# Forgetting attention: two query blocks of a head finished together, one bias operation for all heads, and the shift's sign taken in where it is spread

## The chip, the core and the metric

The kernel runs on one core of one Trainium2 chip. The metric is device time in microseconds for one execution of the whole kernel, as the median of several runs. A core has five engines with a queue of instructions each: TensorE (PE, with its weight loads shown as PEld), VectorE (DVE), ScalarE (ACT), GpSimd (POOL) and SyncE (SP), which issues nearly all DMA transfers of this kernel. Queues run side by side and wait for each other through semaphores.

## The reference

One layer of a streaming encoder. 16 meta tokens are put in front of 2048 input tokens (T = 2064, width 1024). The layer normalises, projects to the inputs of three groups of heads (a linear recurrence, forgetting attention, RWKV-7), joins their outputs by an output projection, and adds a normalised result; then comes a gated feed-forward part with a short convolution. The change lies in the forgetting attention, 8 heads of 64 columns:

```
log_f = log_sigmoid(f_logit + f_bias)
c = cumsum(log_f)                                   # per head, over the tokens
s = q @ k^T / 8 + (c[query] - c[key]),  -inf where key > query
o = softmax(s) @ v
```

## The kernel before

**The stages.** The input projection comes first, in three parts of the tokens, with the recurrences beside it. Then `Attn.run` (lines 771 to 796) does the attention. The end of the last recurrence overlaps with its beginning, and the output projection (`w_out_tile`, line 1443, 17 tiles of up to 128 tokens) overlaps with its second half. The feed-forward part follows. The program is written in one order; the framework then plans each engine's queue from estimated durations (`schedule_with_timeline_sim=True`, line 2141), so that work written later can be put into gaps.

**The attention's blocks.** A block is one head and 512 queries: 8 heads times 4 query blocks b = 0 to 3, 32 blocks, after 16 meta queries that `meta` does apart. The first half of the stage does b = 0 and 1 of all heads, the second half b = 2 and 3; within a half, the two blocks of a head follow each other. Each block has three steps.

`maxima` (line 503) finds, for each of the 512 queries, the largest score. TensorE computes scores in pieces into banks called `mx` (line 527), VectorE reduces each piece (lines 530, 533) and then the pieces of a query (line 540) into `sh`, 128 partitions by 4. Line 541 negates that and subtracts the reference `cref` (the value of `c` at the block's first key tile). TensorE transposes the result (line 545) and `shift` (line 553) spreads it into four rows of the operand `q2`: row j holds the shift of queries 128 j to 128 j + 127 and zeros elsewhere, because it is multiplied with the unit matrix on the way. In the trace `q2` is called `q`. Line 548 makes the block's bias, `cref - ccol` for each of 17 key tiles.

`weights` (line 621) runs two blocks behind. For each tile of 128 keys TensorE computes scores transposed (`sc`, lines 653 and 654; `q2` and `k2` bring in shift and forgetting), ScalarE takes the exponential with the bias (line 658), GpSimd masks, and TensorE multiplies with the values into `po` (line 676). `po` holds two partial sums, in partitions 0 to 63 and 64 to 127. GpSimd and VectorE add up the weights in `acc` (line 697) for the denominators. While it does so, `fill` puts pieces of `maxima` of a later block between.

`ending` (line 702) finishes a block. The two halves of `po` are added into `o`, 64 partitions by 512 (lines 710 to 713). Then three steps are put off by `DELAYS` = 2, 7 and 12 ticks (a tick is a pair of key tiles): `total` sums `acc` over the partitions by matmul and stores 512 denominators to memory (line 726), and reads them back as 16 by 32 (line 727); `invert` takes the reciprocal (line 731), stores it (line 732) and reads it back spread over 64 partitions as `rb` (line 733); `scale` multiplies `o` by `rb` (line 736) and stores it to `scr["mix"]` (line 737), from which the output projection reads. The delayed steps that are still open at the end run after the last block.

**The order around it.** SyncE's queue issues the loads of `q` and `k` of later blocks, these stores and reads, and the loads of the output projection, in the planned order; an issue waits for what it needs and all behind it wait too. Tiles 7 and 8 of the output projection are held back (`HELD`, line 1858) until the last matmul of the second-last block, to have work for TensorE at the end. Tile i (from 1) covers tokens 16 + 128 (i - 1) onwards, so tiles 1 to 8 read blocks b = 0 and 1, tiles 9 to 12 read b = 2 and tiles 13 to 16 read b = 3, of all heads.

Of the kernel before, what the change touches and what calls it, by code (L numbers as in the profile page):

```python
# [8 lines left out]
F32 = mybir.dt.float32  # L9
# [3 lines left out]
AF = mybir.ActivationFunctionType  # L13
ALU = mybir.AluOpType
# [4 lines left out]
P = 128  # L19
# [306 lines left out]
NH = 8  # L326
NKT = 17
# [6 lines left out]
def attn_consts(core):  # L334
    nc = core.nc
    c = core.const

    core.future = c.tile([P, P], F32, name="future")
    nc.gpsimd.memset(core.future[:], 0.0)
    nc.gpsimd.affine_select(  # L340
        out=core.future[:], in_=core.future[:], compare_op=ALU.is_ge, fill=NEG, base=0,
        pattern=[[-1, P]], channel_multiplier=1,
    )
    core.ones_row = c.tile([1, P], F32, name="ones_row")
    nc.vector.memset(core.ones_row[:], 1.0)
    core.ccol = c.tile([P, NKT, NH], F32, name="ccol")
    nc.vector.memset(core.ccol[:], 0.0)
    core.cref = c.tile([P, NKT, NH], F32, name="cref")
    core.ctail = c.tile([NH, META], F32, name="ctail")
    nc.vector.memset(core.ctail[:], 0.0)  # L350
    core.ones_col = c.tile([P, 1], F32R, name="ones_col")
    nc.vector.memset(core.ones_col[:].bitcast(F32), 1.0)
    core.ones_64 = c.tile([META, 64], F32, name="ones_64")
    nc.vector.memset(core.ones_64[:], 1.0)
    core.ones_8 = c.tile([NH, 1], F32, name="ones_8")
    nc.vector.memset(core.ones_8[:], 1.0)

# [54 lines left out]
class Attn:  # L412
# [7 lines left out]
    def __init__(self, core, pool, psum, more, scr):  # L420
        self.core, self.pool, self.psum, self.more, self.scr = core, pool, psum, more, scr
        self.wide, self.bank, self.place = False, 0, 0
        nc = self.nc = core.nc
        self.clock, self.later, self.serial, self.added = 0, [], 0, 0
        self.pending, self.loads, self.steps = None, [], []


        self.turn = {"k": 1, "q2": 0, "q3": 0}
        self.ring = {s: [] for s in self.turn}
        for i in range(self.AHEAD + 1):  # L430
            q3 = pool.tile([P, 512], F32R, tag=f"q3_{i}", name=core.n("q3"), bufs=1)
            self.fixed(q3, None, self.ONES)
            self.ring["q3"].append(q3)
            q2 = pool.tile([P, 512], F32R, tag=f"q2_{i}", name=core.n("q2"), bufs=1)
            nc.vector.memset(q2[64:128].bitcast(F32), 0.0)
            self.ring["q2"].append(q2)
            if i > 1:
                continue
            k1 = pool.tile([P, 2, KHALF], F32R, tag=f"k1_{i}", name=core.n("k1"), bufs=1)
            k2 = pool.tile([P, 2, KHALF], F32R, tag=f"k2_{i}", name=core.n("k2"), bufs=1)  # L440
            v1 = pool.tile([P, 2, NKT // 2 + 1, 64], F32, tag=f"v1_{i}", name=core.n("v1"), bufs=1)
            self.fixed(None, k2, self.ONES)
            self.ring["k"].append((k1, k2, v1))
# [59 lines left out]
    def maxima(self, h, b, keys):  # L503

        nc, core, scr = self.nc, self.core, self.scr
        k1, k2, v1 = keys
        r = slice(64 * h, 64 * h + 64)
        t0, n, ref = META + 512 * b, 512, 4 * b
        qt = [(P * i, P, META + P * (4 * b + i)) for i in range(4)]
        ts = slice(t0, t0 + n)  # L510
        q3 = self.next("q3")
        q1 = self.t([P, 512], "q1", F32R, self.AHEAD + 1)
        q2 = self.next("q2")
        nc.sync.dma_start(q3[0:64, :n].bitcast(F32), scr["qh"][r, ts])
        nc.sync.dma_start(q1[0:64, :n].bitcast(F32), scr["qh"][r, ts])
        nc.sync.dma_start(q1[64:128, :n].bitcast(F32), scr["qh"][r, ts])
        nc.sync.dma_start(q2[0:64, :n].bitcast(F32), scr["ql"][r, ts])
        nq = len(qt)
        mc = self.t([P, 4, 6], "mc")
        nc.vector.memset(mc[:], NEG)  # L520
        for i, (qo, rows, prior) in enumerate(qt):
            for ci in range(len(MAX_CUTS) - 1):
                a, e = MAX_CUTS[ci], min(MAX_CUTS[ci + 1], prior + rows)
                if a >= e:
                    break
                ps = self.mx()
                nc.tensor.matmul(ps[:rows, : e - a], q3[:, qo : qo + rows], k2[:, a:e], start=True, stop=True)  # L527
                full = min(e, prior) - a
                if full > 0:
                    self.reduced = nc.vector.tensor_reduce(mc[:rows, i, ci : ci + 1], ps[:rows, :full], axis=AX.X, op=ALU.max)  # L530
                if e == prior + rows:
                    junk = self.t([P, P], "mj")
                    nc.vector.tensor_tensor_reduce(
                        junk[:rows, :rows], ps[:rows, full : full + rows], core.future[:rows, :rows],
                        1.0, NEG, ALU.add, ALU.max, mc[:rows, i, 5:6],
                    )
                yield None
        sh = self.t([P, 4], "sh")
        rows = qt[0][1]
        nc.vector.tensor_reduce(sh[:rows, :nq], mc[:rows, :nq], axis=AX.X, op=ALU.max)  # L540
        nc.vector.tensor_scalar(
            sh[:rows, :nq], sh[:rows, :nq], -1.0, core.cref[:rows, ref, h : h + 1], op0=ALU.mult, op1=ALU.subtract
        )
        ps = self.mx()
        nc.tensor.transpose(ps[:nq, :rows], sh[:rows, :nq], core.ident[:rows, :rows])
        self.shift(q2.rearrange("p (i q) -> p i q", q=P), ps[:nq, :rows])
        bias = self.t([P, NKT], "bias", bufs=self.AHEAD + 1)
        nc.vector.tensor_scalar(
            bias[:], core.ccol[:, :, h], -1.0, core.cref[:, ref, h : h + 1], op0=ALU.mult, op1=ALU.add
        )  # L550
        yield q1, q2, bias

    def shift(self, q2, rows):

# [66 lines left out]
    def weights(self, h, b, keys, queries, fill):  # L621
# [6 lines left out]
        nc, core, scr = self.nc, self.core, self.scr  # L628
        k1, k2, v1 = keys
        q1, q2, bias = queries  # L630

        t0, n = META + 512 * b, 512
# [69 lines left out]
        def ending(po, acc):  # L702


            while len(self.later) > 8:
                self.later.pop(0)[2]()

            o, oh = self.t([64, 512], "o", bufs=4), self.t([64, 512], "oh")
            c1 = kt[1][2]
            nc.scalar.activation(oh[:, c1:n], po[64:128, c1:n], AF.Copy)  # L710
            if c1:
                nc.scalar.activation(o[:, :c1], po[0:64, :c1], AF.Copy)
            nc.vector.tensor_tensor(o[:, c1:n], po[0:64, c1:n], oh[:, c1:n], op=ALU.add)
            g = n // 16
            dcol = self.t([16, 32], "dcol", bufs=4)
            rb = []

            def total():
                ah, al = (self.t([P, 512], "oh", F32R) for _ in range(2))
                nc.scalar.activation(ah[:, :n], acc[:, :n], AF.Copy)  # L720
                nc.gpsimd.tensor_tensor(al[:, :n], acc[:, :n], ah[:, :n], op=ALU.subtract)
                ps = self.mx()
                nc.tensor.matmul(ps[0:1, :n], core.ones_col[:], ah[:, :n], start=True, stop=False)
                nc.tensor.matmul(ps[0:1, :n], core.ones_col[:], al[:, :n], start=False, stop=True)
                nc.scalar.activation(acc[0:1, :n], ps[0:1, :n], AF.Copy)
                nc.sync.dma_start(scr["den"][h : h + 1, ts], acc[0:1, :n])
                nc.sync.dma_start(dcol[:, :g], scr["den"][h, ts].rearrange("(p c) -> p c", c=g))

            def invert():
                rb.append(self.t([64, 512], "rb"))  # L730
                nc.vector.reciprocal(dcol[:, :g], dcol[:, :g])
                nc.sync.dma_start(scr["rden"][h, ts].rearrange("(p c) -> p c", c=g), dcol[:, :g])
                nc.sync.dma_start(rb[0][:, :n], scr["rden"][h : h + 1, ts].broadcast_to([64, n]))

            def scale():
                nc.vector.tensor_tensor(o[:, :n], o[:, :n], rb[0][:, :n], op=ALU.mult)
                nc.sync.dma_start(scr["mix"][256 + 64 * h : 256 + 64 * h + 64, ts], o[:, :n])

            for d, f in zip(self.DELAYS, (total, invert, scale)):
                self.serial += 1  # L740
                self.later.append((self.clock + d, self.serial, f))
            self.later.sort(key=lambda x: x[:2])
# [1402 lines left out]
```

## Time and profile before

| what | value |
|---|---|
| three runs | 3115.06, 3122.15, 3122.59 us |
| their median | 3122.15 us |
| the profiled execution, its span from first to last instruction | 3106.3 us |
| mean clock granted to TensorE in it | 0.961 |
| the stage of the attention in it | about 875 to 1612 us |

The profile is of one execution. Its own time is its span and what lies around it; the span is 15.85 us below the median of the runs. A line such as "L736 DVE TENSOR_TENSOR o<-o,rb 64x512 f32<-64x512 f32 x32 | busy, mean ns | idle" names the line of the code, the engine, the operation, output and inputs, partitions by elements, the count, then the busy time in us, the mean of one in ns, and the idle time of the engine just before, with what ended it. In a window the columns are its bounds and length, the busy time and count of PE, PEld, DVE, ACT and POOL, the granted clock, the share of the DMA engines and GB/s. In the chain of waits each piece has its start, its length and what it was. Lines of waits give the waiting engine and line, what ended the waits, their sum, number and longest.

### The profile page before, as it was taken

The numbers are of one execution on the slowest core, as the hardware profiler recorded it, in microseconds if no ns is written. First come the engines' busy times: TensorE is split into PE (matmuls) and PEld (weight loads), VectorE is DVE, ScalarE is ACT, GpSimd is POOL, SyncE is SP. The second block draws the span as 40 slices with busy tenths as digits, with TensorE's granted clock in tenths as the row PEclk, the third lists the DMA queues.
The fourth block names the chain that finished last, engine by engine and source line by source line (L and its number), as shares of the span: only waits on it lengthen the run. The fifth ranks groups of instructions, "written<-read, shape, count | busy, mean of one in ns | idle before, by whom it ended". The sixth has DMA issues, their size and how long they took to land.

```text
span 3106.3 us, 52286 instructions
## 1 busy us (share of the span) xinstructions
PE 2921.8 (94%) x18488; PEld 2493.4 (80%) x18488; DVE 2208.1 (71%) x4322; ACT 1463.2 (47%) x2770; POOL 1318.1 (42%) x1436
## 2 busy tenths in 40 slices
PE   6998999999978999999989899999999999999998
PEld 6987988998855664565558899999999999787876
DVE  6248655676688788777745899897778777557766
ACT  4135334344534444445544555566666665324333
POOL 3310101101133465446743568743533334556665
PEclk9999999999977799999999999999999999999999
DMA  6664333353352334444336455565555565535444
GB/s 202 231 205 142 103 89 107 106 150 98 96 139 65 77 90 128 118 125 107 80 101 199 155 180 167 171 197 169 165 168 163 167 188 160 180 102 173 143 166 143
DMA packets 456502, 443.71 MB, mean 143 GB/s; under 512 B 82496, under 2 KB 373514, under 8 KB 453408
## 3 DMA queue, kind: packets, MB, share of 16 engines
q1 hardware_dynamic: 455856, 439.99, 47.8%
q8 instruction: 145, 2.38, 0.3%
q14 instruction: 117, 0.96, 0.1%
q0 software_dynamic: 384, 0.39, 0.0%
HBM read 314.39 MB, written 125.87 MB: 142 GB/s over the span
## 4 chain that ended last, share of the span: by engine, by line
PE 61%; DVE 14%; DMA 12%; POOL 5%; issue 4%; ACT 3%; SPq 0%; POOLq 0%; DVEq 0%; ACTq 0%
PE psu L168 7%; PE psu L169 7%; PE psu L170 7%; PE psp L168 4%; PE psp L169 4%; PE psp L170 4%; PE po L676 3%; PE psd L170 2%; PE psd L168 2%; PE psd L169 2%; DVE uw L1554 2%; PE mx L527 2%; DVE uy L1665 2%; PE sc L653 2%; PE pswo L170 2%
## 5 line engine op out<-in xcount | busy, mean ns | idle before, releaser
L168 PE MATMUL psu<-xo,uw 128*128 128x344 f32 x1848 | 592.1, 324 | 23.5 <-DVE vb L1709 12.5
L169 PE MATMUL psu<-xo,uw 128*128 128x344 f32 x1848 | 594.5, 322 | 0.0
L170 PE MATMUL psu<-xo,uw 128*128 128x344 f32 x1848 | 584.3, 321 | 0.0
L168 PE MATMUL psp<-xh,wh 128*128 128x384 f32 (+2 forms) x1152 | 380.6, 330 | 0.0
L170 PE MATMUL psp<-xh,wl 128*128 128x384 f32 (+2 forms) x1152 | 377.6, 328 | 3.0 <-DVE wl L163 3.0
L169 PE MATMUL psp<-xl,wh 128*128 128x384 f32 (+2 forms) x1152 | 376.7, 327 | 0.0
L168 PEld LDWEIGHTS psu<-xo,uw 128*128 128x128 f32 x1848 | 348.6, 189 | 28.8 <-DVE vb L1709 15.5
L1554 DVE TENSOR_TENSOR uw<-uq,uw 128x512 fp32r<-128x512 f32 x352 | 333.6, 954 | 53.3 <-ACT uw L1553 49.9
L169 PEld LDWEIGHTS psu<-xo,uw 128*128 128x128 f32 x1848 | 349.8, 189 | 0.0
L170 PEld LDWEIGHTS psu<-xo,uw 128*128 128x128 f32 x1848 | 348.1, 189 | 0.0
L1553 ACT ACTIVATE uw<-uq 128x512 fp32r<-128x512 f32 x462 | 286.9, 627 | 90.9 <-PE psu L170 43.2
L658 ACT ACTIVATE p<-sc,bias 128x512 f32<-128x512 f32 (+4 forms) x352 | 197.5, 591 | 218.9 <-PE sc L654 184.1
L1665 DVE SCALAR_TENSOR_TENSOR uy<-psu,ffn_cols,uy 128x342 f32<-128x342 f32 (+1 forms) x396 | 223.7, 567 | 70.5 <-ACT uy L1663 69.6
L697 POOL TENSOR_TENSOR acc<-acc,p 128x512 f32<-128x512 f32 (+3 forms) x208 | 228.5, 1102 | 84.2 <-DVE acc L697 36.5
L1671 POOL TENSOR_TENSOR uy<-uy,uy 128x342 f32<-128x342 f32 (+1 forms) x132 | 145.8, 1105 | 225.4 <-DVE uy L1665 88.9
L170 PEld LDWEIGHTS psp<-xh,wl 128*128 128x128 f32 x1152 | 218.9, 190 | 10.4 <-issue 5.5
L168 PEld LDWEIGHTS psp<-xh,wh 128*128 128x128 f32 x1152 | 218.8, 190 | 7.1 <-issue 4.7
L169 PEld LDWEIGHTS psp<-xl,wh 128*128 128x128 f32 x1152 | 218.7, 190 | 6.7 <-issue 4.3
L1554 POOL TENSOR_TENSOR uw<-uq,uw 128x512 fp32r<-128x512 f32 x110 | 158.7, 1443 | 137.1 <-ACT uw L1553 116.7
L530 DVE TENSOR_REDUCE mc<-mx 128x1 f32<-128x400 f32 (+5 forms) x320 | 171.8, 554 | 57.5 <-PE mx L527 55.7
L1554 DVE TENSOR_TENSOR fo<-u,fo 128x896 fp32r<-128x896 f32 x88 | 106.4, 1209 | 122.3 <-ACT fo L1553 122.3
L1626 POOL TENSOR_TENSOR uq<-uq,uq 128x512 f32<-128x512 f32 x88 | 137.6, 1566 | 113.0 <-DMA uq<-in_ffn_up_dram 96.4
(460 smaller groups left out, 6539.2 us busy)
## 6 DMA issues: line engine op xcount, KB each, us to landing
uq<-in_ffn_up_dram SPq DMA_DIRECT2D x220, 256.0 KB
uq<-scr_us SPq DMA_DIRECT2D x176, 256.0 KB
raw<-in_w_in_dram SPq DMA_DIRECT2D x72, 512.0 KB
scr_us<-uq SPq DMA_DIRECT2D x88, 256.0 KB
u<-scr_ff SPq DMA_DIRECT2D x88, 256.0 KB
scr_ff<-uy SPq DMA_DIRECT2D x110, 171.0 KB
q<-scr_qh SPq DMA_DIRECT2D x96, 128.0 KB
ds<-in_ffn_down_dram SPq DMA_DIRECT2D x10, 1024.0 KB
```

What stands on the lines that cost most here:

```text
L168: nc.tensor.matmul(out, ah, bh, start=first, stop=False, skip_group_check=more)
L169: nc.tensor.matmul(out, ah, bl, start=False, stop=False, skip_group_check=more)
L170: nc.tensor.matmul(out, al, bh, start=False, stop=last, skip_group_check=more)
L530: self.reduced = nc.vector.tensor_reduce(mc[:rows, i, ci : ci + 1], ps[:rows, :full], axis=AX.X, op=ALU.max)
L658: last = nc.scalar.activation(p[:rows, :w], ps[:rows, :w], AF.Exp, bias=bias[:rows, j : j + 1])
L676: mm = nc.tensor.matmul(po[at : at + 64, c0:n], v1[:rows, j], p[:rows, : n - c0], start=start and i < 2, stop=end and i + 2 >= len(group), ...
L697: eng.tensor_tensor(a, ps_[0][0][:rows, c0:n] if start and i == 1 else a, p[:rows, : n - c0], op=ALU.add)
L1553: core.nc.scalar.activation(hi, src, AF.Copy)
L1554: (eng or core.nc.vector).tensor_tensor(lo, src, hi, op=ALU.subtract)
L1626: core.nc.gpsimd.tensor_tensor(raw[:], self.raw[x][:], self.raw[y][:], op=op)
L1665: stt(y[:, :n], src[:, i : n + i], cw[:, 44 * i + cc : 44 * i + cc + 1], y[:, :n], op0=ALU.mult, op1=ALU.add)
L1671: core.pooled = nc.gpsimd.tensor_tensor(v[:, :n], g[:, :n], v[:, :n], op=ALU.mult)
```

## The change

- The shift (in `maxima`): line 541 goes, so the plain maxima are transposed. The spreading operation now adds `cref` and multiplies with the negative unit matrix `minus`, a constant made once.
- The bias: instead of one operation of 17 columns per block there is one of 17 x 8 columns for each b, at its first head, kept to the end of the kernel's attention. It subtracts `ccol` from `cref` for all heads.
- The ending: the two blocks of a head share one tile `o` of 128 partitions, the even b in the lower and the odd b in the upper half, and one tile `dcol` of 16 by 64. `total` runs for each block and stores its denominators, but only the odd block reads them back, both blocks in one. `invert` and `scale` run once per pair: one reciprocal, one store, two reads into the halves of `rb`, one multiplication over 128 partitions and two stores to `scr["mix"]`. The even block has no `invert` and no `scale` of its own; its rows are stored when the odd block's are. `o` has 3 buffers of two blocks instead of 4 of one.

```
@@ -352,6 +352,8 @@
     nc.vector.memset(core.ones_col[:].bitcast(F32), 1.0)
     core.ones_64 = c.tile([META, 64], F32, name="ones_64")
     nc.vector.memset(core.ones_64[:], 1.0)
+    core.minus = c.tile([4, 4], F32, name="minus")
+    nc.vector.tensor_scalar(core.minus[:], core.ident[:4, :4], -1.0, None, op0=ALU.mult)
     core.ones_8 = c.tile([NH, 1], F32, name="ones_8")
     nc.vector.memset(core.ones_8[:], 1.0)
 
@@ -423,6 +425,7 @@
         nc = self.nc = core.nc
         self.clock, self.later, self.serial, self.added = 0, [], 0, 0
         self.pending, self.loads, self.steps = None, [], []
+        self.bias, self.minus = {}, core.minus
 
 
         self.turn = {"k": 1, "q2": 0, "q3": 0}
@@ -538,17 +541,20 @@
         sh = self.t([P, 4], "sh")
         rows = qt[0][1]
         nc.vector.tensor_reduce(sh[:rows, :nq], mc[:rows, :nq], axis=AX.X, op=ALU.max)
-        nc.vector.tensor_scalar(
-            sh[:rows, :nq], sh[:rows, :nq], -1.0, core.cref[:rows, ref, h : h + 1], op0=ALU.mult, op1=ALU.subtract
-        )
         ps = self.mx()
         nc.tensor.transpose(ps[:nq, :rows], sh[:rows, :nq], core.ident[:rows, :rows])
-        self.shift(q2.rearrange("p (i q) -> p i q", q=P), ps[:nq, :rows])
-        bias = self.t([P, NKT], "bias", bufs=self.AHEAD + 1)
-        nc.vector.tensor_scalar(
-            bias[:], core.ccol[:, :, h], -1.0, core.cref[:, ref, h : h + 1], op0=ALU.mult, op1=ALU.add
+        four = [nq, nq, rows]
+        nc.vector.scalar_tensor_tensor(
+            q2[64 : 64 + nq].rearrange("p (i q) -> p i q", q=P),
+            ps[:nq, :rows].rearrange("i (o q) -> i o q", o=1).to_broadcast(four), core.cref[:nq, ref, h : h + 1],
+            self.minus[:].rearrange("i (j o) -> i j o", o=1).to_broadcast(four), op0=ALU.add, op1=ALU.mult,
         )
-        yield q1, q2, bias
+        if h == 0:
+            self.bias[b] = self.t([P, NKT, NH], f"bias{b}", bufs=1)
+            nc.vector.tensor_tensor(
+                self.bias[b][:], core.cref[:, ref : ref + 1].to_broadcast([P, NKT, NH]), core.ccol[:], op=ALU.subtract
+            )
+        yield q1, q2, self.bias[b][:, :, h]
 
     def shift(self, q2, rows):
 
@@ -705,14 +711,18 @@
             while len(self.later) > 8:
                 self.later.pop(0)[2]()
 
-            o, oh = self.t([64, 512], "o", bufs=4), self.t([64, 512], "oh")
+            side = b % 2
+            if side == 0:
+                self.two = self.t([P, 512], "o", bufs=3), self.t([16, 64], "dcol")
+            o, dcol = self.two
+            oh = self.t([64, 512], "oh")
+            mine = o[64 * side : 64 * side + 64]
             c1 = kt[1][2]
             nc.scalar.activation(oh[:, c1:n], po[64:128, c1:n], AF.Copy)
             if c1:
-                nc.scalar.activation(o[:, :c1], po[0:64, :c1], AF.Copy)
-            nc.vector.tensor_tensor(o[:, c1:n], po[0:64, c1:n], oh[:, c1:n], op=ALU.add)
-            g = n // 16
-            dcol = self.t([16, 32], "dcol", bufs=4)
+                nc.scalar.activation(mine[:, :c1], po[0:64, :c1], AF.Copy)
+            nc.vector.tensor_tensor(mine[:, c1:n], po[0:64, c1:n], oh[:, c1:n], op=ALU.add)
+            both = slice(t0 - n, t0 + n)
             rb = []
 
             def total():
@@ -724,19 +734,24 @@
                 nc.tensor.matmul(ps[0:1, :n], core.ones_col[:], al[:, :n], start=False, stop=True)
                 nc.scalar.activation(acc[0:1, :n], ps[0:1, :n], AF.Copy)
                 nc.sync.dma_start(scr["den"][h : h + 1, ts], acc[0:1, :n])
-                nc.sync.dma_start(dcol[:, :g], scr["den"][h, ts].rearrange("(p c) -> p c", c=g))
+                if side:
+                    nc.sync.dma_start(dcol[:], scr["den"][h, both].rearrange("(p c) -> p c", c=64))
 
             def invert():
-                rb.append(self.t([64, 512], "rb"))
-                nc.vector.reciprocal(dcol[:, :g], dcol[:, :g])
-                nc.sync.dma_start(scr["rden"][h, ts].rearrange("(p c) -> p c", c=g), dcol[:, :g])
-                nc.sync.dma_start(rb[0][:, :n], scr["rden"][h : h + 1, ts].broadcast_to([64, n]))
+                rb.append(self.t([P, 512], "rb"))
+                nc.vector.reciprocal(dcol[:], dcol[:])
+                nc.sync.dma_start(scr["rden"][h, both].rearrange("(p c) -> p c", c=64), dcol[:])
+                for i in range(2):
+                    cs = slice(t0 - n * (1 - i), t0 + n * i)
+                    nc.sync.dma_start(rb[0][64 * i : 64 * i + 64], scr["rden"][h : h + 1, cs].broadcast_to([64, n]))
 
             def scale():
-                nc.vector.tensor_tensor(o[:, :n], o[:, :n], rb[0][:, :n], op=ALU.mult)
-                nc.sync.dma_start(scr["mix"][256 + 64 * h : 256 + 64 * h + 64, ts], o[:, :n])
-
-            for d, f in zip(self.DELAYS, (total, invert, scale)):
+                nc.vector.tensor_tensor(o[:], o[:], rb[0][:], op=ALU.mult)
+                for i in range(2):
+                    cs = slice(t0 - n * (1 - i), t0 + n * i)
+                    nc.sync.dma_start(scr["mix"][256 + 64 * h : 256 + 64 * h + 64, cs], o[64 * i : 64 * i + 64])
+
+            for d, f in zip(self.DELAYS, (total, invert, scale) if side else (total,)):
                 self.serial += 1
                 self.later.append((self.clock + d, self.serial, f))
             self.later.sort(key=lambda x: x[:2])
```

## Prediction

> **What bounds the kernel now.** I read the page first (busy shares, clock slices, the chain of work that ended last), then the stage in which the change lies.
>
> ```profile
> PE 2921.8 (94%) x18488; PEld 2493.4 (80%) x18488; DVE 2208.1 (71%) x4322; ACT 1463.2 (47%) x2770; POOL 1318.1 (42%) x1436
> PE 61%; DVE 14%; DMA 12%; POOL 5%; issue 4%; ACT 3%; SPq 0%; POOLq 0%; DVEq 0%; ACTq 0%
> ```
>
> TensorE is the bound over the whole span. The changed lines run from 874.6 us (first bias, row below) to the last scaling near 1612, so the next rows are of 875 to 1600 us: the stage as one window, its first 375 us, and the longest waits there.
>
> ```profile
> 875.00:1600.00 725.00, 659.86 (x3951) 409.49 (x3950) 561.19 (x1478) 337.39 (x648) 393.00 (x497) 0.90 0.40 99
> 875.00:1250.00 375.00, 331.12 (x2539) 211.55 (x2537) 304.52 (x870) 167.40 (x345) 183.34 (x267) 0.83 0.41 101
> ```
> ```profile
> PE mx L527 <- DVE mc L530: 10.1, 11, 3.5
> PE mx L527 <- DVE mc L533: 8.6, 8, 2.2
> PE mx L527 <- DVE q L556: 5.4, 5, 1.7
> PE sc L653 <- ACT p L658: 10.5, 26, 1.4
> ACT p L658 <- PE sc L654: 184.1, 129, 8.7
> DVE mc L530 <- PE mx L527: 55.7, 64, 3.3
> ```
>
> PE is busy 659.86 of 725 us, so at most some 65 us of shown idleness is to be had. VectorE (third column) is the second engine with 561.19 us, 77%. What PE waits for from VectorE is its `mx` banks: 10.1 + 8.6 + 5.4 = 24.1 us. In the other direction VectorE waits 55.7 us for PE. Both hand work back and forth through two or three banks, so time taken off VectorE counts only where VectorE is the later one. The chain of waits says how often that is: its VectorE pieces between 875 and 1600 us are 363, together 152.15 us; these are the first and the last.
>
> ```profile
> 875.25 0.18 DVE mq L568
> ...
> 1594.10 0.61 DVE wx L1482
> ```
>
> 152.15 of 561.19 busy: 0.27 of a microsecond of VectorE work lies on the chain here.
>
> **What the change does to VectorE.** The costs come from the groups by line and from the range of durations of single lines:
>
> ```profile
> L736 DVE TENSOR_TENSOR o<-o,rb 64x512 f32<-64x512 f32 x32 | 30.8, 975 | 9.3 <-DMA rb<-scr_rden 9.3
> L556 DVE TENSOR_TENSOR q<-mx,ident 4x512 fp32r<-4x512 f32 x32 | 21.8, 682 | 3.6 <-PE mx L545 2.7
> L541 DVE TENSOR_SCALAR sh<-sh,cref 128x4 f32<-128x4 f32 x32 | 13.4, 418 | 0.4
> L548 DVE TENSOR_SCALAR bias<-ccol,cref 128x17 f32<-128x17 f32 x32 | 11.7, 368 | 3.9 <-ACT p L658 3.9
> L731 DVE RECIPROCAL dcol<-dcol 16x32 f32<-16x32 f32 x32 | 10.3, 329 | 17.8 <-DMA dcol<-scr_den 17.7
> ```
> ```profile
> L1481 DVE SCALAR_TENSOR_TENSOR pswo<-pswo,rs,g_post 128x512 f32<-128x512 f32 (+1 forms) x16 | 11.3, 748 | 0.2
> L1482 DVE TENSOR_TENSOR wx<-wx,pswo 128x512 f32<-128x512 f32 (+1 forms) x16 | 10.5, 672 | 0.0
> ```
> ```profile
> L541 DVE TENSOR_SCALAR sh<-sh,cref x32: 207/230/1341, 887.3 to 1557.5; 128x4 f32<-128x4 f32 x32
> L548 DVE TENSOR_SCALAR bias<-ccol,cref x32: 124/232/1235, 874.6 to 1527.6; 128x17 f32<-128x17 f32 x32
> L736 DVE TENSOR_TENSOR o<-o,rb x32: 666/802/1746, 984.1 to 1611.9; 64x512 f32<-64x512 f32 x32
> ```
>
> The sign (L541) goes in all 32 blocks: 13.4 us. The bias (L548) goes: 11.7 us. The scaling (L736) runs 16 times on 128 partitions with the same 512 elements in each: half of 30.8, 15.4 us. The reciprocal runs 16 times over 64 instead of 32 columns. A wide one costs between 329 and 2 x 329 ns; I take 0.5 us, 8.0 in all, so 2.3 us are saved (0 to 5).
>
> Added: the spread of the shift becomes a three-operand operation with a scalar from a column. The nearest row is L1481, also out of PSUM with a column scalar and 512 elements: 748 against 682 ns, 32 x 0.066 = 2.1 us. Four bias operations of 136 columns: the rows have 0.23 us for 17 (median of L548) and 0.672 for 512 (L1482), so about 0.34 each, 1.4 us; the ends are 0.12 and 1.24 each (shortest and longest L548). The constant `minus` is one operation of 4 columns, nothing.
>
> Work: 13.4 + 11.7 + 15.4 + 2.3 - 2.1 - 1.4 = 39.3 us less. Waits in the VectorE queue go as well. A bias had to wait until ScalarE was through with the one three blocks back, and every reciprocal stood behind a round trip through memory; these two rows are of 875 to 1570 us, the first all gone, the second half:
>
> ```profile
> DVE dcol L731 <- DMA dcol<-scr_den: 4.2, 3, 2.3
> DVE bias L548 <- ACT p L658: 3.9, 5, 1.3
> ```
>
> 3.9 + 2.1 = 6.0 us. Of 45.3 us freed, 0.27 reaches the end: 12.2 us. That is the value I take. The ends: if only PE's shown waits count, 24.1 of 561.19, it is 45.3 x 0.043 = 2 us; and more than the 24.1 us that PE waits for VectorE can hardly be won.
>
> The means of L541, L548 and L736 (418, 368, 975) lie far above their medians (230, 232, 802): some wait inside for something that takes a GpSimd add's length. [...] By medians 13.4, 11.7 and 15.4 become 7.4, 7.4 and 12.8, the total 45.3 becomes 32, and the gain 8.7 instead of 12.2.
>
> **The queue of transfers.** Each block issues den out, dcol in, rden out, rb in, mix out. Of the 32 dcol reads and 32 rden writes 16 remain; den, rb and mix keep 32. SyncE's queue stands still between a write and the read of it:
>
> ```profile
> SPq L727 <- DMA scr_den<-acc: 22.7, 22, 2.6
> SPq L733 <- DMA scr_rden<-dcol: 23.2, 21, 3.3
> ```
>
> So half of about 46 us of standing goes, and with it delays of the q and k loads queued behind. What one such round trip is worth is seen at one place, on the chain and on PE:
>
> ```profile
> 1507.49 3.91 DMA scr_den<-acc
> 1511.46 4.62 DMA dcol<-scr_den
> ```
> ```profile
> 1517.25 0.57 PE L527 MATMUL mx<-k,q 128*128 128x512 f32 x1 [2.25 <-DVE mc L533]
> ```
>
> 8.5 us of chain, but PE stood still only 2.25 us. With half of the round trips gone I take 2 us (0 to 8.5). Body together: 14 us less, ends 2 and 25.
>
> **What comes later.** The even block of a head now waits for the odd one before its reciprocal and scaling. Its reciprocal, its rb load and its mix store move behind the odd block's in the queues of VectorE and SyncE. In the middle of the stage I cost that at nothing: the output-projection tiles 1 to 8 that read these rows are spread as filler among the attention matmuls of the second half; without that cover it would be one tile's 11.5 us (below). At the end it does matter. Projection tile 9 is the first to need query block 2 of all heads:
>
> ```profile
> 1586.51 0.45 SPq L737 DMA_DIRECT2D scr_mix<-o  x1
> 1588.73 0.39 SPq L161 DMA_DIRECT2D raw<-scr_mix  x1
> 1612.58 0.45 SPq L737 DMA_DIRECT2D scr_mix<-o  x1
> ```
> ```profile
> 1597.08 0.50 PE L168 MATMUL pswo<-woh,mh 128*128 128x512 f32 x1 [1.87 <-ACT mh L162]
> 1620.18 0.65 PE L1520 MATMUL pst<-ident,xt 2*128 2x2 f32 x8
> 1631.26 0.78 PE L168 MATMUL pswo<-woh,mh 128*128 128x512 f32 x1
> ```
> ```profile
> 1620.00:1635.00 15.00, 8.36 (x38) 6.44 (x37) 14.96 (x22) 8.46 (x20) 6.75 (x4) 0.66 0.90 275
> ```
> ```profile
> 1235.21 4.57 DMA raw<-in_w_out_dram
> 1595.97 0.97 ACT mh L162
> ```
>
> Now the block-2 store leaves at 1586.51 and the load of tile 9 2.22 us later; tiles 8 and 9 fill PE from 1597.08 to 1620.18, 11.5 us each. After the change both stores stand at 1612.58 and 0.45 later. The load follows at about 1615.3, lands 4.57 later (a load of the same 512 KB) and is split by 1620.8. So PE has tile 8 until 1608.6 and nothing for 12.2 us. But before, PE had a hole of its own behind tile 9: from 1620 to 1635 it was busy 8.36 of 15 us, and tile 10 began at 1631.26. Tile 9 now falls into that hole, 1620.8 to 1632.3, and tile 10 is late by 1 us, or by 6 with the transposes of the hole (some 4.5 us) in front of it. I take 4 us later, ends 0 and 12.
>
> **Sum.** 14 less, 4 more: 10 us less. The profiled execution spans 3106.3 us, 15.85 below the median of the runs, 3122.15; 3096.3 + 15.85 = 3112.15 us, taken as 3112.
>
> **Rivals.** (1) No change. VectorE already waits 55.7 us for PE, and ScalarE 184.1 us: freed time would only lengthen these waits. The body gives 2 to 5, the end takes 4: 3122 us. Against it: the 24.1 us that PE waits for VectorE.
>
> (2) A larger gain through the clock. In 875 to 1250 us the granted clock is 0.83, and from 1620 to 1635, where PE stands still half of the time, 0.66. If shorter VectorE work closes PE's gaps, PE also runs faster: from 0.83 to 0.88 its 331.12 us shrink by 19, half of it on the path, say 10 more: 3102 us. [...] Against it: much of the low clock there sits beside the recurrence's small matmuls, which stay.
>
> (3) Slower, by the end of the stage. If the load of tile 9 stands in SyncE's queue behind other loads, or the transposes do not fit in, the 12.2 us of idle PE stay whole, and at a clock of 0.66 the 15 us behind them lose another 5: 17 later, 12 net of a body of 5, 3134 us. It decides from a start of tile 9 after about 1625 (on before's time scale) together with a small body gain. For it: nothing else of size is ready for PE then. Against it: the hole that tile 9 fills.
>
> **Chances.** 0.3% of the median, 9.4 us, is about what a measurement can tell here. The forecast gets 0.42: it sits near that bound, so 0.28 of it counts as faster, 0.14 as the same. Rival 1 gets 0.27 (0.24 same, 0.03 slower: each engine's queue order is planned anew from estimated durations, which can cost some microseconds anywhere), rival 2 0.18 (faster), rival 3 0.13 (slower). Faster 0.46, same 0.38, slower 0.16. Low end: body 25, end 4 and part of rival 2: 3094. High end: rival 1 with a bad order, half-way to rival 3: 3128. The likeliest case by itself reaches from 3104 to 3118.
>
> **What would show it.** Right: L541's 32 operations gone, four of 136 columns, scaling 16 times below 1 us each, VectorE some 39 us less busy in the stage, PE's waits on `mc` and `q` below 24.1 us, the last attention matmul some 14 us before 1595. The spread at about 0.75 us. The end: an empty PE between tile 8 and tile 9, and less of a hole after it. Wrong: VectorE's busy time falls while its waits for PE rise by as much (rival 1); the clock of the first 375 us goes above 0.86 (rival 2); tile 10 starts more than 10 us later after the last attention matmul than now (rival 3).

## The result, and the profile after

The changed kernel takes 3099.14 us (median of 22 runs, 3086.69 to 3115.19) against 3113.74 us for the kernel before in 22 runs on the same chip. The ratio is 0.9945 with a 95% interval of 0.9932 to 0.9958: 0.55% of 3113.74, so 17 us faster (13 to 21); the two medians alone differ by 14.6. The profiled executions don't show this by their spans: 3106.3 us before, 3104.7 us after, and 3106.40 us is the time of that same run of after, near the slow end of its 22. The change has to be read from the stage's rows and from the experiments, not from the two spans.

The page of after first, in the lines that answer to the two shown of before:

```profile
PE 2923.7 (94%) x18488; PEld 2496.3 (80%) x18488; DVE 2167.8 (70%) x4231; ACT 1462.1 (47%) x2770; POOL 1302.0 (42%) x1436
PE 63%; DVE 12%; DMA 11%; POOL 6%; issue 4%; ACT 3%; SPq 1%; POOLq 0%; DVEq 0%; ACTq 0%
```

VectorE is 2208.1 - 2167.8 = 40.3 us less busy. Its share of the chain falls from 14% to 12%, TensorE's rises from 61% to 63%. Next the windows of the stage in after (columns as in the prediction: PE, PEld, DVE, ACT, POOL, granted clock, transfers):

```profile
875.00:1600.00 725.00, 659.80 (x3948) 414.54 (x3949) 519.06 (x1381) 337.18 (x646) 385.61 (x497) 0.90 0.39 98
875.00:1250.00 375.00, 335.84 (x2543) 217.72 (x2545) 285.07 (x821) 166.95 (x343) 178.72 (x267) 0.81 0.41 100
```

VectorE's third column went from 561.19 to 519.06, 42.1 us; TensorE and the clock of the stage are the same. The groups by line of after, 870 to 1615 us, and the range of the bias operation:

```profile
L547 DVE SCALAR_TENSOR_TENSOR q<-mx,cref,minus 4x512 fp32r<-4x512 f32 x32 | 23.7, 741 | 9.4 <-PE mx L545 8.7
L749 DVE TENSOR_TENSOR o<-o,rb 128x512 f32<-128x512 f32 x16 | 14.1, 883 | 8.0 <-DMA rb<-scr_rden 8.0
L742 DVE RECIPROCAL dcol<-dcol 16x64 f32<-16x64 f32 x16 | 8.5, 534 | 6.2 <-DMA dcol<-scr_den 6.1
```
```profile
L554 DVE TENSOR_TENSOR bias<-cref,ccol x4: 270/282/300, 873.7 to 877.8; 128x136 f32<-128x136 f32 x4
```

The spread (741 ns, 748 taken) and the wide reciprocal (534, 500 taken) are close to the forecast; the scaling (883, half of 30.8 us in 16 makes 963) and the bias (282, 340 taken) cost less than forecast. The waits of after in the stage show where the freed time went in part:

```profile
PE mx L530 <- DVE mc L533: 10.2, 11, 2.9
PE mx L530 <- DMA k<-scr_cl: 7.6, 4, 3.4
PE mx L530 <- DVE mc L536: 4.2, 5, 1.7
PE mx L530 <- DVE q L547: 1.7, 2, 1.2
DVE mc L533 <- PE mx L530: 66.7, 53, 4.7
```

TensorE's waits on `mc` and `q` fell from 24.1 to 16.1 us. A new row is the second one: score pieces wait 7.6 us for the last load of their key operand `k2`, the low part of `c` (`scr_cl`). VectorE's wait for TensorE rose from 55.7 to 66.7 us.

### The profile page after: what moved, and what is told of

The parts are those of the page before. It is cut to its first block, busy times and chain, and to the rows that moved or that the text cites. A ratio compares the mean times of both kernels' runs of the same rounds, so it can differ in the third digit from the quotient of the medians.

```text
span 3104.7 us, 52180 instructions
## 1 busy us (share of the span) xinstructions
PE 2923.7 (94%) x18488; PEld 2496.3 (80%) x18488; DVE 2167.8 (70%) x4231; ACT 1462.1 (47%) x2770; POOL 1302.0 (42%) x1436
## 4 chain that ended last, share of the span: by engine, by line
PE 63%; DVE 12%; DMA 11%; POOL 6%; issue 4%; ACT 3%; SPq 1%; POOLq 0%; DVEq 0%; ACTq 0%
PE psu L168 7%; PE psu L169 7%; PE psu L170 7%; PE psp L169 4%; PE psp L170 4%; PE psp L168 4%; PE po L682 3%; PE psd L169 2%; PE psd L168 2%; PE psd L170 2%; PE pswo L168 2%; PE pswo L170 2%; PE pswo L169 2%; DVE uw L1569 2%; PE mx L530 2%
## 5 line engine op out<-in xcount | busy, mean ns | idle before, releaser
L168 PE MATMUL psu<-xo,uw 128*128 128x344 f32 x1848 | 592.7, 325 | 23.3 <-DVE vb L1724 11.7
L533 DVE TENSOR_REDUCE mc<-mx 128x1 f32<-128x400 f32 (+6 forms) x320 | 172.3, 555 | 70.0 <-PE mx L530 66.7
L1641 POOL TENSOR_TENSOR uq<-uq,uq 128x512 f32<-128x512 f32 x88 | 129.5, 1473 | 117.0 <-DMA uq<-in_ffn_up_dram 82.6
```

What stands on the lines that cost most here:

```text
L168: nc.tensor.matmul(out, ah, bh, start=first, stop=False, skip_group_check=more)
L1641: core.nc.gpsimd.tensor_tensor(raw[:], self.raw[x][:], self.raw[y][:], op=op)
```

## The experiments

The theory at this point was that of the prediction: time freed on VectorE counts by one share, whatever the operation (0.27, or a larger one). Rivals: the halved round trips carry the gain; the common ending carries it; the waits and not the work of the bias carry it; the freed time is partly lost to waits for key loads; or the framework, which plans all queues anew for every edit, happened on a better plan. The expectations below call the first theory W, that of the round trips Q and that of the plan P; M and S are told where they come up. Times are against the kernel before on the same chip.

**The kernel before once more** (`null_before`), to see what no change looks like.

> The kernel before once more, unchanged, against itself. Every theory expects a ratio of 1.000 within 0.002. It shows how far single executions of one kernel scatter, and whether their time follows the clock that was granted to TensorE: if it does, executions with a mean clock 0.01 lower are some 20 us longer (the slope of the 22 executions of the changed kernel is 1873 us per unit of mean clock).

3109.78 us, ratio 0.9997 [0.9978, 1.0015].

**Sign and bias without the common ending** (`sign_bias`): the part of the diff in `maxima`, with `ending` as before.

> Before, with only the sign taken in with the spread and the bias of all heads in one operation; every block ends by itself as before. Theory W (freed VectorE time is what counts, about 0.35 us per us freed): these two free some 22 us of work and 4 us of waits of the 45 in all, so 8 us of the 16 are won: ratio 0.997 to 0.998. Theory Q (the halved round trips through memory and the standing of SyncE's queue count): next to nothing, 0.9995 to 1.0005. Theory P (a luckier plan of the queues counts): any value, and the two parts of the change don't add up to the whole.

3196.61 us, ratio 1.0273 [1.0247, 1.0299]: 85 us slower, which only theory P, with its "any value", didn't exclude. The window of its first 125 us in the stage, the first key maximum on TensorE, and then before's window:

```profile
875.00:1000.00 125.00, 100.81 (x962) 82.19 (x959) 68.92 (x196) 41.87 (x93) 18.15 (x37) 0.51 0.09 19
```
```profile
1094.09 0.64 PE L530 MATMUL mx<-k,q 128*128 128x144 f32 x2
```
```profile
875.00:1000.00 125.00, 104.27 (x736) 68.74 (x735) 102.94 (x298) 53.68 (x112) 42.13 (x72) 0.71 0.41 99
880.44 0.78 PE L527 MATMUL mx<-k,q 128*128 128x144 f32 x2 [4.83 <-issue]
```

Attention begins at 1094 instead of 880 us, after the recurrence instead of beside it; alone, the recurrence's small matmuls run at a granted clock of 0.51. The compiled program's addresses point to the reason. The recurrence's pool begins at byte 125,600 of each partition, and the attention's pool ends at 124,736 before, 124,608 after, but at 126,656 here: the four bias tiles (136 floats, 544 bytes each) need more than the room between. In the changed kernel the common ending pays for them, since it holds three buffers of `o` of 2,048 bytes instead of four. Here the pools overlap, and attention waited until the recurrence was done: in this trace the recurrence's last VectorE operation ends at 1085.1 us, and the first memset of an attention operand (`q`, line 452) starts at 1085.3.

**The common ending alone** (`pair_only`): the part of the diff in `ending`, with sign and bias as before.

> Before, with only the common ending of the two blocks of a head. Theory W: 18 us of VectorE work and 2 us of waits freed, 7 us won, ratio 0.9975 to 0.9985. Theory Q: nearly the whole gain, 0.9945 to 0.9955. Theory P: any value.

3115.59 us, ratio 1.0011 [0.9991, 1.0031]: nothing, though its stage has VectorE 24.5 us less busy than before (561.19):

```profile
875.00:1600.00 725.00, 656.91 (x3941) 410.17 (x3941) 536.74 (x1438) 335.40 (x644) 382.42 (x495) 0.90 0.40 97
```
```profile
PE mx L527 <- DMA k<-scr_cl: 14.5, 6, 3.3
PE mx L527 <- DVE mc L533: 5.7, 5, 2.1
PE mx L527 <- DVE mc L530: 5.3, 5, 2.7
PE mx L527 <- DVE q L556: 1.2, 2, 1.0
```

TensorE's waits for VectorE fell from 24.1 to 12.2 us here, more than in after, and 14.5 us of waits for keys stand in their place.

**The VectorE work put back into the changed kernel** (`dve_back`), into tiles nobody reads: the 32 sign and 32 bias operations, and each scaling a second time (the tiles' own lines left out, each operation put in one line):

```
+        nc.vector.tensor_scalar(idle[:, :4], sh[:], -1.0, core.cref[:, ref, h : h + 1], op0=ALU.mult, op1=ALU.subtract)
+        nc.vector.tensor_scalar(idle[:, 4:], core.ccol[:, :, h], -1.0, core.cref[:, ref, h : h + 1], op0=ALU.mult, op1=ALU.add)
...
+                nc.vector.tensor_tensor(idle[:], o[:], rb[0][:], op=ALU.mult)
```

> The changed kernel with the saved VectorE work put back as work that nobody waits for: per block one 128x4 and one 128x17 operation with a scalar column, per pair one more multiplication 128x512, all into tiles that nothing reads. Round trips stay halved. Theory W: VectorE is some 38 us busier than in the changed kernel, and nearly the whole gain is lost, ratio to the kernel before 0.998 to 1.000. Theory Q: the gain stays, 0.9945 to 0.996.

3215.01 us, ratio 1.0335 [1.0313, 1.0357]. It says nothing on the question: its tiles take the attention's pool to 126,752, and the first key maximum stands at 1093.93 us, as in `sign_bias`. Both were made again so that the pools fit.

**Sign and bias, fitted** (`sign_bias_fit`): as `sign_bias`, with two bias tiles used in turn (the pool ends at 125,568).

```
-            self.bias[b] = self.t([P, NKT, NH], f"bias{b}", bufs=1)
+            self.bias[b] = self.t([P, NKT, NH], f"bias{b % 2}", bufs=1)
```

> The sign and the bias alone once more, now with two bias tiles that the second half of the heads uses again, so that the attention's tiles end at byte 125,568 of a partition and not at 126,656; the recurrence's tiles begin at 125,600. Theory M (the 85 us of the first try came from memory: the attention could not start before the recurrence had given its tiles back) expects the attention to start near 880 us again and a ratio of at most 1.002. What is left is then the worth of the two edits: theory W (freed VectorE time counts wherever it is) 0.997 to 0.998; theory S (the small operations count for more than their length, since they wait inside behind GpSimd and stand in the row from the maxima to the shift) 0.993 to 0.996, that is all the gain, as the common ending alone gave none; theory P (the plan) anything from 0.998 to 1.003.

3087.68 us, ratio 0.9929 [0.9907, 0.9952]: 22 us faster, at least all of the gain, without the common ending. Theory M holds: attention begins near 880 us again.

```profile
876.76 0.78 PE L530 MATMUL mx<-k,q 128*128 128x144 f32 x2 [4.94 <-issue]
```

It is the fastest kernel made here by its ratio, but the intervals of this and of the changed kernel overlap, so neither can be called the better.

**The sign alone** (`sign_only`): the bias per block as before.

> Before, with only the sign taken in with the spread; bias per block and every block by itself. Theory W: 11 us of VectorE work net, ratio 0.998 to 0.9995. Theory S: half or more of the gain, 0.995 to 0.998, since this operation stood between the maxima and the transpose. Theory P: anything from 0.998 to 1.003.

3106.13 us, ratio 0.9993 [0.9974, 1.0012]: nothing to be seen.

**The work put back, fitted** (`dve_back_fit`): as `dve_back`, with the second pass of the scaling done on `rb` in place (`rb` max `rb`).

> The changed kernel with the saved VectorE work put back, this time within the memory (the attention's tiles end at 124,704): per block a 128x4 and a 128x17 operation that nobody waits for, per pair one more operation of 128x512 on rb (its maximum with itself) ahead of the scaling. Theory W: VectorE again some 38 us busier, the gain is lost, ratio 0.998 to 1.000. Theory S: a third to a half is lost, 0.996 to 0.998. Theory Q or a gain that lies in the order alone: it stays, 0.994 to 0.9955.

3115.46 us, ratio 1.0008 [0.9990, 1.0026]. The whole gain is gone, though the halved round trips and the common ending are still there: it goes with the operations on VectorE.

**The round trips put back** (`trips_back`): the changed kernel with a read of denominators and a store of reciprocals per block, VectorE's work unchanged.

```
+                nc.sync.dma_start(dcol[:, side], scr["den"][h, ts].rearrange("(p c) -> p c", c=32))
...
+                    nc.sync.dma_start(scr["rden"][h, cs].rearrange("(p c) -> p c", c=32), dcol[:, i])
```

> The changed kernel, but each block again reads its own denominators back and has its own store of reciprocals: 32 reads of dcol and 32 stores of rden instead of 16 each, in the two halves of one dcol tile, all VectorE work as in the changed kernel. If the halved round trips carry part of the gain (my prediction gave them 2 us of 14), the ratio rises from 0.9945 by 0.0005 to 0.001; theory Q: to 0.998 or above; if they carry nothing: 0.9935 to 0.9955.

3087.65 us, ratio 0.9937 [0.9914, 0.9960], as the changed kernel. The 32 transfers saved carry nothing that can be measured; the two intervals leave room for 6 us, so the 2 us of the prediction are not refuted by it.

**The bias alone** (`bias_fit`), fitted as above, the sign operation kept.

> Bias edit alone (two bias tiles used in turn, so that the attention pool ends below the recurrence pool); sign operation and single endings as before. If freed VectorE time counts by its share of the chain: 11.7 - 1.4 + 3.9 us of waits = 14.2 us, times 0.27 = 4 us less, ratio 0.999. If the bias edit carries the gain of sign and bias together: some 20 us less, ratio 0.993. If both edits are needed: in between, about 0.996 to 0.998.

3102.63 us, ratio 0.9971 [0.9952, 0.9990]: 9 us (3 to 15). Between the cases: twice what a share of 0.27 gives, and less than both edits together. 2 (sign) and 9 make 11, together they gave 22; the intervals (about 6 us each way for each) leave open whether the two really help each other.

**The bias' wait without its work** (`sign_bufs`): the sign edit, and the 32 bias operations with 8 buffers instead of 3, so that they needn't wait for ScalarE.

```
-         bias = self.t([P, NKT], "bias", bufs=self.AHEAD + 1)
+         bias = self.t([P, NKT], "bias", bufs=8)
```

> Sign edit, and the 32 bias operations kept but with 8 buffers instead of 3, so that they no longer wait for ScalarE: takes away the wait of the bias edit without its work. If that wait (VectorE's queue stands behind it) is what the bias edit is worth: some 20 us less, ratio 0.993. If the work of the 32 operations is what it is worth: as the sign edit alone, ratio 0.9993; by shares 3.9 x 0.27 = 1 us less.

3114.27 us, ratio 1.0014 [0.9996, 1.0032]. It isn't faster than the sign alone (0.9993), so the wait isn't what the bias edit gains by. The wait isn't gone wholly: 1.5 us are left in this profile, 3.2 in that of `sign_only`. What remains for the bias edit are the operations that it removes.

**Only the small operations put back** (`small_back`): `dve_back` without its second scaling.

> The changed kernel with the 32 sign and 32 bias operations put back into a tile that nobody reads; endings in pairs, wide scaling. If freed time counts by amount whatever the operation: 25.1 of 45.3 us back, 17 us less becomes about 8 less, ratio 0.9975. If the small operations carry all of the gain: ratio 1.000. If the scaling in 128 partitions carries it: as the changed kernel, 0.9945.

3113.01 us, ratio 1.0007 [0.9992, 1.0021]: all of the gain is gone with the 64 small operations alone. Its ranges by line:

```profile
L545 DVE TENSOR_SCALAR idle<-sh,cref x32: 209/246/1973, 886.2 to 1553.5; 128x4 f32<-128x4 f32 x32
L548 DVE TENSOR_SCALAR idle<-ccol,cref x32: 209/252/2191, 871.7 to 1533.7; 128x17 f32<-128x17 f32 x32
```

Medians of a quarter of a microsecond, maxima of 2: 64 of these take back some 19 us (17 from the gain, 2 beyond it; the two intervals make it about 13 to 25). By their rows they are busy 17.4 and 20.7 us here, 38.1 in all and not the 25.1 of before, while VectorE as a whole is busy 2194.3 - 2167.8 = 26.5 us more than in after.

**The key loads out of the way** (`after_late`): the changed kernel with the two `k1` loads of a head (260 KB each in the first half of the stage, 516 in the second) moved to where its values are loaded (the first two heads excepted).

```
-        nc.sync.dma_start(k1f[0:64, :n], scr["kh"][r, :n])
-        nc.sync.dma_start(k1f[64:128, :n], scr["kl"][r, :n])
         def values():
+            nc.sync.dma_start(k1f[0:64, :n], scr["kh"][r, :n])
+            nc.sync.dma_start(k1f[64:128, :n], scr["kl"][r, :n])
```

> The changed kernel with the two loads of k1 (258 KB each) put off from the start of a head to where its values are loaded, so that the low parts of the next head's key maxima no longer queue with them. If part of the freed time is lost to waits for these loads: TensorE's 7.6 + 2.2 us of waits for key loads go, some 8 us less than the changed kernel, ratio about 0.992. If these waits only stand in place of others: as the changed kernel, 0.9945.

3092.33 us, ratio 0.9940 [0.9917, 0.9964], not to be told from the changed kernel's 0.9945. Its waits in the stage:

```profile
PE mx L537 <- DVE mc L540: 12.5, 14, 2.9
PE mx L537 <- DVE mc L543: 3.8, 6, 1.1
PE mx L537 <- DMA k<-scr_cl: 2.2, 3, 0.9
```

The wait for `scr_cl` fell from 7.6 to 2.2 us as meant, and the one on `mc` rose from 10.2 to 12.5. So the new row of waits in after isn't a loss that can simply be won back; and that it swallowed the gain of `pair_only`, as its 14.5 us suggest, isn't shown. `sign_bufs` has 1.3 us of this wait and no gain either.

## Why the prediction was right, and where its steps were not

**Work freed: right.** 39 us forecast, 42.1 us in the stage's window and 40.3 over the whole execution. The spread and the reciprocal came within 0.04 us of what was taken, the scaling and the bias were 0.08 and 0.06 us cheaper.

**The share of 0.27: right in sum, wrong as a rule.** The step took every freed microsecond alike. By it the bias (11.7 - 1.4, and 3.9 of waits) is worth 3.8 us, the sign (13.4 - 2.1) 3.1, and scaling, reciprocal and their waits (15.4 + 2.3 + 2.1) 5.3. The runs have 22 us (15 to 29) for sign and bias, and nothing for the common ending: alone (`pair_only`, 3 us slower, from 3 faster to 10 slower), added to sign and bias (0.9945 against 0.9929), or with the scaling's time put back beside the small operations (1.0008 against 1.0007). That the 12.2 us came out near the measured number is luck: one kind of operation was taken too low and the other too high. The prediction's second figure, by medians, is an estimate that leaves out the time by which some of these operations run longer than the rest; its 8.7 us instead of 12.2 aren't borne out: with the medians alone the small operations would have been worth less than by their means, and they were worth more than either. The long ones go with GpSimd in the trace of before: the 20 of the 64 that took over 0.3 us each ended 0.02 to 0.04 us after a GpSimd operation that ran beside them. In `small_back` the 64 operations are busy 38.1 us by their rows and VectorE as a whole 26.5 us more than in after, so its other operations are 11.6 us less busy; whether waits passed from these to the 64 isn't shown.

The kernels side by side, with VectorE's busy time from each profile's page:

| kernel | 32 sign operations | 32 bias operations | endings | VectorE, us | ratio |
|---|---|---|---|---|---|
| before, again (`null_before`) | yes | yes | single | 2208.1, 2206.3 | 0.9997 |
| `dve_back_fit` | yes | yes | pairs, scaling time back | 2208.2 | 1.0008 |
| `small_back` | yes | yes | pairs | 2194.3 | 1.0007 |
| `bias_fit` | yes | no | single | 2191.3 | 0.9971 |
| `sign_only` | no | yes | single | 2189.2 | 0.9993 |
| `pair_only` | yes | yes | pairs | 2183.7 | 1.0011 |
| `sign_bufs` | no | yes | single | 2183.1 | 1.0014 |
| `sign_bias_fit` | no | no | single | 2176.7 | 0.9929 |
| `trips_back` | no | no | pairs | 2169.3 | 0.9937 |
| after | no | no | pairs | 2167.8 | 0.9945 |
| `after_late` | no | no | pairs | 2162.3 | 0.9940 |

All four kernels without either kind of small operation have the whole gain, the one without the bias operations alone has a part of it, and no kernel that keeps the 32 bias operations gains anything that can be seen. So regular a sorting speaks against theory P, though each kernel has a plan of its own. But the same four also have the least VectorE work. A step in the amount, nothing up to 25 us freed and all of it from 31 us on, would sort them nearly as well; only `bias_fit` speaks against it, with 9 us from 17 us freed where `pair_only` and `sign_bufs` have none from 24 and 25. The amounts are of single profiles, which differ by 2 us between the two of before. No run frees 31 us or more by other operations, so kind and amount aren't parted for good.

The chain could not have told them apart either. After the change VectorE's pieces on it between 875 and 1600 us are 361 with 145.94 us, of 519.06 busy: again 0.28. These are the first and the last:

```profile
875.71 0.50 DVE q L453
...
1594.60 0.70 DVE o L724
```

The share didn't fall when 42 us were taken off the engine, so it isn't the price of an operation. TensorE's shown waits for VectorE don't price it either: on `mc` and `q` they are 24.1 us before and 16.1 after, but 12.2 in `pair_only`, without a gain, and 10.7 + 3.7 + 3.0 = 17.4 in `sign_bias_fit`, with the largest.

**Where the 64 operations stand** doesn't explain their weight. In before's code the sign lies between the last reduction of a block's maxima and TensorE's transpose (lines 540, 541, 545), in the path by which a block's scores can begin; the bias follows the spread, and the scaling is put off by ticks, with nothing on TensorE that reads it until the output projection. In the planned queue the bias isn't there: the prediction's rows have the bias operations from 874.6 to 1527.6 us and the signs from 887.3 to 1557.5, and by the trace each block's bias starts 14 to 62 us before its spread. And the path doesn't fit the runs. From the last reduction to the transpose it takes 2.46 us before (mean of 32 blocks in the trace) and 1.34 in `sign_only`, which gains nothing; in `small_back`, where nothing reads what the 64 operations write, it takes 1.77 us, less than the 2.32 of after, and the gain is gone. So the place in that path isn't the reason, and the runs show no other.

**Bias buffers and round trips: no gain to be seen.** There is none from the 3.9 us of waits for ScalarE (`sign_bufs`) and none from the halved round trips, for which 2 us were taken (`trips_back`); amounts of 1 or 2 us lie below what these runs can tell. SyncE's waits for these stores did fall, from 45.9 us to 32.9:

```profile
SPq L746 <- DMA scr_rden<-dcol: 18.7, 13, 2.8
SPq L738 <- DMA scr_den<-acc: 14.2, 12, 2.6
```

`trips_back` has all the transfers again and is no slower (0.9937 against 0.9945), but of the standing only 3 us came back (23.1 + 12.8 = 35.9 us). So it shows that the number of transfers doesn't count here, and not what the standing is worth.

**The end of the stage: forecast 4 us later, measured 0.5.** The last attention matmuls, SyncE's queue, tile 9, and the first matmul of the feed-forward part, in after:

```profile
1588.86 3.46 PE L682 MATMUL po<-p,v 128*64 128x512 f32 x18
1606.94 1.10 SPq L752 DMA_DIRECT2D scr_mix<-o  x2
1609.25 0.39 SPq L161 DMA_DIRECT2D raw<-scr_mix  x1
1614.59 0.50 PE L168 MATMUL pswo<-woh,mh 128*128 128x512 f32 x1 [4.22 <-ACT mh L162]
1620.00:1635.00 15.00, 14.66 (x74) 11.72 (x73) 11.49 (x20) 7.62 (x19) 7.18 (x5) 1.00 0.88 278
1700.36 0.32 PE L168 MATMUL psu<-xo,uw 128*128 128x344 f32 x1
```

and the same two ends before:

```profile
1591.75 3.46 PE L676 MATMUL po<-p,v 128*64 128x512 f32 x18
1702.73 0.32 PE L168 MATMUL psu<-xo,uw 128*128 128x344 f32 x1
```

From the end of the last `po` to the feed-forward part it is 1700.36 - 1592.32 = 108.04 us after and 1702.73 - 1595.21 = 107.52 before. TensorE is empty for 4.22 us ahead of tile 9, not for 12.2: the last stores leave at 1606.94, not at 1612.58, since the last matmul is 2.9 us earlier and the stores follow it 14.6 instead of 17.4 us later. The other half held: tile 9 falls into before's hole, where TensorE is now busy 14.66 of 15 us (8.36 before) at a clock of 1.00 (0.66). Rival 3's condition, a start of tile 9 after about 1625, wasn't met (1614.59).

**What lies around the span.** The forecast added 15.85 us, before's median less its profiled span. The profiled run of after has a span of 3104.7 and a time of 3106.40: 1.7 us lie around it. The rest of the 15.85 was the profiled run against the median of three others; with 22 runs before's median is 3113.74. The forecast of 3112 is so 13 us above the measured 3099.14, of which 8.4 (3122.15 - 3113.74) come from the median of three, and the other 4.6 from a gain taken too small, 10 against 14.6 by medians. The measured time lies inside the range of 3094 to 3128, but below the 3104 to 3118 of the likeliest case. One sign named for being right failed: the last attention matmul ends 2.9 us earlier in the profile and not some 14. That profile lies 7.3 us above the median of its kernel, so it shows little of the gain.

**The rivals.** Rival 1 holds for one part: VectorE's waits for TensorE did rise by 11 us, and the common ending alone makes no change. But in `pair_only` these waits are 57.1 us against 55.7, so it isn't they that took its freed time. Rival 2 isn't borne out in the profile of after, whose first 375 us have a clock of 0.81, below before's 0.83. It may have a part in `sign_bias_fit`: its profiled run and the sign alone have

```profile
875.00:1250.00 375.00, 335.42 (x2644) 215.76 (x2644) 302.79 (x874) 176.95 (x363) 193.88 (x280) 0.90 0.44 107
```
```profile
875.00:1250.00 375.00, 340.22 (x2525) 217.51 (x2527) 287.38 (x827) 166.13 (x340) 178.69 (x265) 0.80 0.39 96
```

The clock is 0.90 against 0.80, and TensorE does 2644 instead of 2525 matmuls in the same time. Whether a denser queue raised the clock, or this one execution (3079.95 us, the fastest of its six) met a better one, a single profile can't say. The mean clocks of all runs on that chip say how much goes with the clock: 0.9645 in the 6 runs of `sign_bias_fit`, 0.9641 in the 7 of `trips_back` and 0.9609 in the 24 of before, whose times fall by 1758 us per unit of clock. By that slope, an estimate, some 6 of their 22 and 20 us go with the clock, and the rest doesn't. Which of the two drives the other stays open.

**What stays open:** why 17.7 us of scaling and reciprocal show no gain while 64 small operations (25.1 us before, 38.1 us put back) are worth some 19, and whether it is their kind, their number or a step in the total of VectorE's work.

## What to carry to other kernels

The share of an engine's time on the chain, 0.27 before and 0.28 after here, didn't price an operation: put the suspected operations back where nothing reads them and see whether the gain goes. Here 64 operations with a median of a quarter of a microsecond weighed some 19 us, which neither that share nor their place in the code foretold. Before a change adds a tile, see how much room its pool has to the next one that is alive at the same time; here 1,056 bytes too many cost 85 us, more than all edits won. Where runs of one kernel spread by 0.9%, compare medians of many runs, not two profiled spans.

## What the runs showed of the hardware that was not expected

The spread of the runs mostly goes with the granted clock, which differs from run to run of the same program: the 22 runs of after have mean clocks from 0.957 to 0.968, and their times correlate with it by -0.80; in the 29 runs of before on the last chip it is -0.87. It isn't always so: -0.21 in the 12 runs of `sign_bufs`, and one run of before with a mean clock of 0.918 took an ordinary 3114.44 us. The profiled run of after has a clock of 0.957, the lowest of its 22, and is 7.3 us above their median; that of before, with the same 1.7 us around its span, is 5.7 below its own. So two spans 1.6 us apart stand for two medians 14.6 us apart:

```profile
core 0: 3104.7 us, clock 0.957
```
```profile
core 0: 3106.3 us, clock 0.961
```

In `sign_bias` TensorE was busy 100.81 of 125 us between 875 and 1000, and yet the granted clock was 0.51: here 81% busy by the profile, with the recurrence's small matmuls, went with half the clock, where before's window of the same time has 0.71 at 104.27 us busy. No run here parts the small matmuls from the gaps between them.
